# Gate and up of a ConvFFN as seven block products (Strassen) on normalised activations, with u and the residual stored to DRAM before the down product

## The chip, the cores and the metric

The kernel runs on one core of one Trainium2 chip. The metric is device time in microseconds (us) of one execution. The profile of an execution names the engines PE (TensorE matmul), PEld (its weight load), DVE (VectorE), ACT (ScalarE), POOL (GpSimd) and SP (SyncE, which here issues all DMAs, in one order).

## The reference

One decoder layer for 1024 prompt positions and 8 sequences of 8 new positions. Both are carried side by side as N = 1088 columns of a transposed activation: eight tiles of 128 model rows by 1088 columns (D = 1024). All arithmetic is fp32. Cut to what matters here:

```python
x = x + concat([a, o], -1) @ w_out            # a: convolution heads, o: attention heads
h = rms_norm(x, norm_ffn_g)
g_full = concat([ffn_past, h @ w_ffn_gate], 1)
g = depthwise_conv_valid(g_full, ffn_conv_w, ffn_conv_b)      # width 3, causal
x = x + (silu(g) * (h @ w_ffn_up)) @ w_ffn_down               # D_FF = 2816
y = rms_norm(x, norm_final_g)
```

The last two rows of `g_full` of each sequence are an output too (`cf`).

## The kernel before

**Matmuls.** An fp32 product is made of three passes in a rounded fp32 type (`F32R`): each operand is split into hi (a rounded copy, made on ACT) and lo (operand minus hi), and hi·hi, hi·lo and lo·hi are added up in PSUM. `gemm` (L154) does this with a weight tile of 128 output rows: for each of three chunks of columns (`CHUNKS`: 384, 384, 320) and each of the `nk` tiles of 128 input rows there are three matmuls (L167, L168, L169), a triple. After a chunk an eviction is called.

**Weights.** `load_w` (L134) loads a raw weight tile by a DMA from SP (L138; tag WR, two buffers), makes hi on ACT (L141) and lo on POOL (L143). hi and lo come from one set of five buffers (tag W); a buffer is free when the last matmul that reads it is done.

**Output projection.** `out_part` (L764) multiplies `mixed` (attention and convolution outputs, kept in DRAM) by `w_out` in three parts of the input rows (`PARTS`: 3, 3 and 2 tiles). Each part loads its tiles of `mixed` (`load_mixed`, L234), splits them on ACT (L237) and DVE (L238), and adds its product from PSUM to the residual tiles `x2` (L779, DVE). The third part is called at L811.

**Norm.** Behind it `scaled_split` (L223) makes hi (L226, ACT) and lo (L228, DVE) of `x2` times the norm's gain, `h2` (L814), and `sum_squares` and `rstd` (L177) make the norm's column factor `R2` (L815): sums over the partitions on PE (L184), the reciprocal root on DVE and ACT (L188 to L199), transposes back on PE (L206) and a copy on ACT (L208). `R2` is multiplied in when gate and up are evicted from PSUM, so the gate product starts on `h2` before `R2` exists.

**FFN.** `ffn_tile(j)` (L821) does 128 of the 2816 FFN rows: gate weights and up weights by `load_w`, gate product, eviction times `R2` (L833, L835), three taps of the convolution on DVE (L843, L846), silu on ACT (L848), up product, eviction (L855), product (L872, L873), and the split of u (hi on ACT L875, lo on DVE L877). u stays in SBUF as hi and lo. `down` (L880) multiplies a group of up to three such tiles by `w_down` for all eight rows of model tiles and adds it to `x2` (L886). The loop at L910 goes over the groups `QSPLIT` (3, 3, 3, 3, 3, 2, 2, 3) and puts the down product of each group behind the first tile of the next. The last group's product (`last_product`, L924) runs column chunk by column chunk (`TAIL`), with the final norm (`last_norm`, L945) and the stores behind it.

**What sets the order.** The program is written in one sequence. A list scheduler decides from it, with its own model of durations, the order of the instructions of each engine; each engine then runs its list strictly in order. Tags of pools hand out buffers in turn, and an instruction that needs a buffer waits until its last readers are done.

In the branch for the convolution heads earlier in the kernel, the taps (`conv_steps`, L326, L328) run on DVE while POOL splits weights; the prediction takes prices from there.

## Time and profile before

| | us |
|---|---|
| median of 3 runs | 1441.66 |
| lowest, highest | 1438.82, 1442.91 |
| the profiled execution, device time | 1440.49 |
| its span in the profile | 1438.7 |

The mean granted TensorE clock over the profiled execution was 0.987 of full speed. In the page's 40 slices of the span (36 us each) the busy tenths are as follows; the FFN begins in slice 18 of 40.

```profile
PE   7989999999999999999999999999999999999995
DVE  7398695566674666586534534534544544544467
ACT  5312111557564564252111111111111111111134
POOL 3221112010010016132223223223223223232235
PEclk9999999999999999999999999999999999999997
DMA  7237676656698785221112012012011011120203
```

A row of a timeline reads: start in us, duration in us, engine, line, operation, output tile <- input tiles, shape, and in brackets what the engine waited for ahead of it. A row of the costliest groups reads: line, engine, operation, output <- inputs and shapes, count | busy time in all in us, mean ns of one | idle time ahead of them, by what ended it. In a table by stage each pair after the length is busy time and count of PE, PEld, DVE, ACT and POOL; then come the granted clock, the DMA engines' mean busy share, and the GB/s they moved.

### The profile page before, as it was taken

To read this page: it belongs to the slowest core of one execution; us is meant where nothing else is said; L and a number is where in the kernel's file an instruction comes from. 1 tells how busy PE (TensorE), PEld (TensorE's weight loads), DVE (VectorE), ACT (ScalarE), POOL (GpSimd) and SP (SyncE) were. 2 spreads that over 40 slices of the span, in tenths; PEclk is the share of its full clock that TensorE was granted. 3 is DMA by queue.
4 is the path that set the end of the run, shared out by engine and by line. 5 is a ranking of instruction groups with operands and counts; after the bars stand their busy time and mean duration, and the time that the engine had idled before them with its cause. 6 is when DMAs were issued, how large, how long until landed. Compare 5 with 4: busy or idle time off the path is not lost.

```text
span 1438.7 us, 23412 instructions
## 1 busy us (share of the span) xinstructions
PE 1391.2 (97%) x9408; PEld 1327.0 (92%) x9408; DVE 817.3 (57%) x1631; ACT 430.1 (30%) x887; POOL 344.5 (24%) x297
## 2 busy tenths in 40 slices
PE   7989999999999999999999999999999999999995
PEld 7989889999977778999999999999999999999995
DVE  7398695566674666586534534534544544544467
ACT  5312111557564564252111111111111111111134
POOL 3221112010010016132223223223223223232235
PEclk9999999999999999999999999999999999999997
DMA  7237676656698785221112012012011011120203
GB/s 270 61 131 266 223 261 195 189 159 178 174 273 251 214 241 204 82 75 38 31 43 66 25 43 73 18 48 68 18 56 60 18 57 37 41 70 11 70 29 125
DMA packets 75340, 161.64 MB, mean 112 GB/s; under 512 B 12000, under 2 KB 46176, under 8 KB 75232
## 3 DMA queue, kind: packets, MB, share of 16 engines
q1 hardware_dynamic: 75232, 160.15, 36.2%
q8 instruction: 74, 1.21, 0.3%
q14 instruction: 34, 0.28, 0.1%
HBM read 128.32 MB, written 31.81 MB: 111 GB/s over the span
## 4 chain that ended last, share of the span: by engine, by line
PE 84%; DVE 9%; DMA 4%; issue 1%; ACT 1%; SPq 1%; POOL 1%; POOLq 0%; DVEq 0%; ACTq 0%
PE g L167 23%; PE g L169 23%; PE g L168 22%; DVE cacc L326 4%; PE o L659 3%; PE s L574 3%; PE t L642 2%; DVE cacc L328 1%; DMA kk<-dk 1%; PE ss L493 1%; DVE qkv L374 1%; DMA cr<-in_kc 1%; DVE xl L228 1%; PE ss L467 1%; PE g L930 1%
## 5 line engine op out<-in xcount | busy, mean ns | idle before, releaser
L167 PE MATMUL g<-xh,wh 128*128 128x384 f32 x1528 | 502.2, 329 | 1.7 <-DVE x L779 1.7
L168 PE MATMUL g<-xl,wh 128*128 128x384 f32 x1528 | 501.0, 328 | 0.0
L169 PE MATMUL g<-xh,wl 128*128 128x384 f32 x1528 | 498.8, 328 | 0.0
L143 POOL TENSOR_TENSOR wl<-wr,wh 128x1024 fp32r<-128x1024 f32 (+3 forms) x148 | 243.4, 1645 | 880.2 <-PE g L169 742.5
L141 ACT ACTIVATE wh<-wr 128x1024 fp32r<-128x1024 f32 (+3 forms) x150 | 112.8, 752 | 602.1 <-PE g L169 481.1
L167 PEld LDWEIGHTS g<-xh,wh 128*128 128x128 f32 x1528 | 288.0, 189 | 3.4 <-ACT wh L141 1.9
L169 PEld LDWEIGHTS g<-xh,wl 128*128 128x128 f32 x1528 | 287.6, 188 | 2.0 <-issue 1.8
L168 PEld LDWEIGHTS g<-xl,wh 128*128 128x128 f32 x1528 | 288.1, 189 | 1.1 <-issue 1.0
L886 DVE TENSOR_TENSOR x<-g,x 128x384 f32<-128x384 f32 x168 | 89.4, 534 | 117.6 <-PE g L169 115.6
L168 PE MATMUL g<-al,wh 128*128 128x384 f32 (+1 forms) x456 | 149.5, 328 | 0.0
L167 PE MATMUL g<-ah,wh 128*128 128x384 f32 (+1 forms) x456 | 149.5, 328 | 0.0
L169 PE MATMUL g<-ah,wl 128*128 128x384 f32 (+1 forms) x456 | 147.3, 328 | 0.0
L833 DVE TENSOR_TENSOR gb<-g,rb 128x384 f32<-128x384 f32 (+1 forms) x66 | 33.6, 512 | 139.5 <-PE g L169 134.7
L615 ACT ACTIVATE y<-y,m 128x128 f32<-128x128 f32 (+1 forms) x192 | 88.4, 463 | 33.7 <-DVE m L603 33.7
L855 DVE TENSOR_TENSOR u<-g,rb 128x384 f32<-128x384 f32 (+1 forms) x66 | 35.1, 533 | 109.8 <-PE g L169 109.8
L578 DVE CUSTOM_DVE_ANT_0 y<-s,pmk 128x128 f32<-128x128 f32 (+1 forms) x192 | 63.9, 378 | 43.1 <-PE s L574 34.1
L167 PEld LDWEIGHTS g<-ah,wh 128*128 128x128 f32 x456 | 85.8, 188 | 0.0
L168 PEld LDWEIGHTS g<-al,wh 128*128 128x128 f32 x456 | 85.7, 188 | 0.0
L169 PEld LDWEIGHTS g<-ah,wl 128*128 128x128 f32 x456 | 85.5, 188 | 0.0
L326 DVE SCALAR_TENSOR_TENSOR cacc<-gp,prm,cacc 128x1024 f32<-128x1024 f32 x60 | 79.9, 1332 | 0.1
L374 DVE TENSOR_TENSOR qkv<-g,rb 128x384 f32<-128x384 f32 (+1 forms) x53 | 41.1, 775 | 46.1 <-PE g L169 46.0
L167 PE MATMUL g<-mh,wh 128*128 128x384 f32 (+1 forms) x192 | 64.1, 345 | 1.7 <-ACT mh L237 1.7
(197 smaller groups left out, 1925.1 us busy)
## 6 DMA issues: line engine op xcount, KB each, us to landing
cr<-in_kc SPq DMA_DIRECT2D x24, 768.0 KB, 8.7
cr<-in_vc SPq DMA_DIRECT2D x24, 768.0 KB, 7.1
kk<-dk SPq DMA_DIRECT2D x48, 256.0 KB, 7.1
wr<-in_w_in SPq DMA_DIRECT2D x22, 512.0 KB, 5.0
wr<-in_w_gate SPq DMA_DIRECT2D x22, 512.0 KB, 3.5
wr<-in_w_up SPq DMA_DIRECT2D x22, 512.0 KB, 3.5
wr<-in_w_down SPq DMA_DIRECT2D x40, 192.0 KB, 2.3
qs<-dq SPq DMA_DIRECT2D x24, 256.0 KB, 4.1
```

The lines of the kernel that those rows point to most:

```text
L141: nc.scalar.activation(hi, raw, AF.Copy)
L143: lo_eng.tensor_sub(lo, raw, hi.bitcast(F32))
L167: nc.tensor.matmul(ps[c], whi[:, k, :], xh[:, t0:t0 + n], start=(k == 0), stop=False)
L168: nc.tensor.matmul(ps[c], whi[:, k, :], xl[:, t0:t0 + n], start=False, stop=False)
L169: nc.tensor.matmul(ps[c], wlo[:, k, :], xh[:, t0:t0 + n], start=False, stop=(k == nk - 1))
L326: eng.scalar_tensor_tensor(acc[:, :S], gp[:, j:j + S], col(w0 + j), acc[:, :S], op0=ALU.mult, op1=ALU.add)
L374: nc.vector.tensor_mul(by_class(x)[:, t0 // 4:(t0 + m) // 4, :], ps[:, :m].rearrange("p (j c) -> p j c", c=4), R[:, t0:t0 + m].rearrange(" ...
L574: nc.tensor.matmul(ps[:, o:o + n], qq, k[a], start=(a == 0), stop=(a == 1))
L578: nc.vector.tensor_tensor_reduce(out=y[:, o:o + n], in0=ps[:, o:o + n], in1=mask, op0=ALU.add, op1=ALU.min, scale=1.0, scalar=3e38, accum_ ...
L615: nc.scalar.activation(y, y, AF.Exp, bias=m[:, 4 * g + i:4 * g + i + 1], scale=-1.0, accum_out=den[:, g, 2 * hd + u, i:i + 1])
L659: done[x].append(nc.tensor.matmul(dst, v, m, start=not done[x], stop=(left[x] == 0)).ins)
L886: nc.vector.tensor_add(x[:, t0:t0 + n], ps[:, :n], x[:, t0:t0 + n])
```

## The change

Three things change.

**Gate and up by seven products.** Rows and columns are cut in two halves: FFN tile j and tile j + 11 are the two row blocks of the weights A, the first and last four tiles of the model rows their column blocks, and the 1088 columns are two halves of 544 (`HN`). With B the normalised activation, Strassen's method in Winograd's form takes, for a pair of tiles, seven products of blocks in place of eight: b11·a11, t2·s2, b21·a12, t1·s1, t3·s3, b22·s4 and t4·a22, with sums and differences t1 to t4 of the activation's blocks, made once, and s1 to s4 of the weights' blocks, made for each pair (`weight_blocks`: four DVE sums). `block_product` runs one product as 2 chunks of 272 columns x 4 tiles x 3 matmuls into a PSUM pair of two banks (four such pairs). Partial results are added up in PSUM or, with the copies `ta` and `tb`, at eviction on DVE (`put`, `put_u`). The gate's first tap goes from DVE to ACT.

**The norm is multiplied in ahead.** The third part of the output projection runs by column halves (`out_half`: half 0 of all eight tiles, then half 1), with its own weights held whole, and `mixed` loaded in halves. Squares go to ACT, their sums to POOL and DVE. `scale_half` multiplies `x2` by the gain and the norm's factor on DVE. The blocks are split, hi on ACT, lo on POOL (b11, b21, b22, t1, t4) or on DVE (t2, t3).

**u and x2 pass through DRAM.** Each finished `x2` half is stored to DRAM (`x2d`) and each finished tile of u too (`ud`). The down product follows as a phase of its own in four groups of `GROUPS` (6, 6, 6 and 4 tiles of u): `load_act` loads and splits u anew, `reload` brings x2 back, and `load_last` loads the last group's weights. Pools F and D replace pool F, and `rstd`'s column of ones is 128 x 1.

```diff
-QSPLIT = (3, 3, 3, 3, 3, 2, 2, 3)
+GROUPS = ((0, 3), (3, 3), (6, 3), (9, 2))
+HN = N // 2
+HF = NF // 2
+PO = 240
...
-        out_part(*load_part(PARTS[-1], zbig, lambda s: zt("F", "X", 16, s, N, F32R)))
-        h2 = [scaled_split(x2[k], col(C_GFFN + k)) for k in range(KT)]
-        R2 = rstd(sum_squares(x2, nc.vector, zbig), D, zbig)
+        def block_product(o, w, x, start):
+            whi, wlo = w
+            nk = len(x)
+            for c in range(2):
+                n = HN // 2
+                ps = o[:, PO:512] if c == 0 else o[:, 512:PO + HN]
+                for k, (xh, xl) in enumerate(x):
+                    t = slice(c * n, c * n + n)
+                    nc.tensor.matmul(ps, whi[:, k, :], xh[:, t], start=(start and k == 0), stop=False,
+                                     skip_group_check=True)
+                    nc.tensor.matmul(ps, whi[:, k, :], xl[:, t], start=False, stop=False, skip_group_check=True)
+                    nc.tensor.matmul(ps, wlo[:, k, :], xh[:, t], start=False, stop=(k == nk - 1),
+                                     skip_group_check=True)
...
+        def out_half(h):
+            acc = [None, None]
+            c = slice(h * HN, h * HN + HN)
+            for i, m in enumerate(order):
+                ps = pair()
+                block_product(ps, wl[m], part[h], True)
+                x = x2[m][:, c]
+                nc.vector.tensor_add(x, all_of(ps), x)
+                nc.sync.dma_start(x2d[m][:, c], x)
+                s = slot("t1", "sq", F32)
+                nc.scalar.activation(s, x, AF.Square)
...
+        def scale_half(h, sq):
+            r = rstd(sq, D, lambda s: slot("b22", s, F32), HN)
+            for k in order:
+                x = x2[k][:, h * HN:h * HN + HN]
+                nc.vector.scalar_tensor_tensor(x, x, col(C_GFFN + k), r, op0=ALU.mult, op1=ALU.mult)
+                if h == 0:
+                    tag = "b11" if k < 4 else "b21"
+                    blocks[tag].append(split(x, tag, nc.gpsimd))
+        sq0 = out_half(0)
+        scale_half(0, sq0)
+        scale_half(1, out_half(1))
+        for k in range(4):
+            (x11, x12), (x21, x22) = halves(x2[k]), halves(x2[k + 4])
+            nc.vector.tensor_sub(x11, x12, x11)
+            blocks["b22"].append(split(x22, "b22", nc.gpsimd))
+            nc.vector.tensor_sub(x12, x22, x12)
+            nc.vector.tensor_sub(x22, x22, x11)
+            nc.vector.tensor_sub(x21, x21, x22)
+            blocks["t2"].append(split(x22, "t2", nc.vector))
+            blocks["t1"].append(split(x11, "t1", nc.gpsimd))
+        for k in range(4):
+            blocks["t3"].append(split(halves(x2[k])[1], "t3", nc.vector))
+            blocks["t4"].append(split(halves(x2[k + 4])[0], "t4", nc.gpsimd))
...
+        def weight_blocks(w, j):
...
+            g, u = raw(j), raw(j + HF)
+            a11, a12 = parts(g, [zt("F", "WA", 2, "wa", D, F32R) for _ in range(2)])
+            t = wide("w22")
+            a22, = parts(u[:, half:], (t[:, :half], t[:, half:]))
+            g1, g2, u1, u2 = g[:, :half], g[:, half:], u[:, :half], u[:, half:]
+            nc.vector.tensor_add(u2, u1, u2)
+            nc.vector.tensor_sub(u1, g1, u1)
+            nc.vector.tensor_sub(g1, u2, g1)
+            nc.vector.tensor_sub(g2, g2, g1)
+            s2, s4 = parts(g, [wide("s24") for _ in range(2)])
+            s3, s1 = parts(u, [wide("s31") for _ in range(2)])
+        def products(w, j, c11, put):
+            a11, a12, a22, s1, s2, s3, s4 = weight_blocks(w, j)
+            x, y = pair("px"), pair("py")
+            block_product(x, a11, blocks["b11"], True)
+            ta = zt("F", "tmp", 4, "ta", HN)
+            nc.scalar.activation(ta, all_of(x), AF.Copy)
+            block_product(y, s2, blocks["t2"], True)
+            put(1, 0, y, ta)
+            block_product(x, a12, blocks["b21"], False)
+            c11(x)
+            block_product(y, s1, blocks["t1"], False)
+            tb = zt("F", "tmp", 4, "tb", HN)
+            nc.vector.tensor_add(tb, all_of(y), ta)
+            z = pair("pz")
+            block_product(z, s3, blocks["t3"], True)
+            put(1, 1, z, tb)
+            block_product(y, s4, blocks["b22"], False)
+            put(0, 1, y, ta)
+            block_product(z, a22, blocks["t4"], False)
+            put(1, 0, z, None)
...
-            nc.vector.tensor_scalar(cvt[:, :W], gb[:, 0:W], col(C_FW + 3 * j), col(C_FB + j),
-                                    op0=ALU.mult, op1=ALU.add)
+                nc.scalar.activation(c[:, :W], gb[i][:, 0:W], AF.Identity, bias=col(C_FB + f), scale=col(C_FW + 3 * f))
...
+                    nc.sync.dma_start(ud[j], u[0])
...
+        def load_act(j0, n):
+            act = []
+            for i in range(2):
+                for j in range(j0 + i * HF, j0 + i * HF + n):
+                    raw = zt("D", "XR", XF, "ur")
+                    nc.sync.dma_start(raw, ud[j])
+                    hi, lo = wide("ah", F32R), wide("al", F32R)
+                    nc.scalar.activation(hi, raw, AF.Copy)
+                    nc.vector.tensor_sub(lo, raw, hi.bitcast(F32))
+                    act.append((hi, lo))
+            return act
```

Where the instructions stand now, at the places that the prediction speaks of. A row is line, operation, output <- inputs, shape; numbers behind a name tell tiles apart.

PE at the FFN's norm, before: `g` is a gate or up product in PSUM, `r` the norm's sums.

```order
L169 MATMUL g_7063<-xh_6878,wl_6971 128x384
L184 MATMUL r_6921<-ones,sqa_6898 128x1 x8
L184 MATMUL r_6921<-ones,sqa_6898 64x1
L167 MATMUL g_7063<-xh_6882,wh_6969 128x384
L168 MATMUL g_7063<-xl_6884,wh_6969 128x384
```

PE there in the change: `g_6789` is the last row block of half 0 of the output projection, `g_6875` the first of half 1.

```order
L841 MATMUL g_6789<-mh_6641,wl_6631 128x272
L189 MATMUL g_1258_6808<-ones,sq_6680 128x1 x4
L189 MATMUL g_1258_6808<-ones,sq_6680 32x1
L211 MATMUL g_1263_6826<-ident,rr_6818 128x128 x4
L211 MATMUL g_1264_6832<-ident,rr_6818 128x32
L838 MATMUL g_6875<-mh_6647,wh_6623 128x272
```

The norm's passes stood between gate matmuls; now half 0's stand, in one piece, ahead of half 1's first matmul.

DVE at the same place in the change: `rb_6825` is half 0's norm factor, the L902 rows are its multiplications into `x2`, the L887 rows the evictions of half 1.

```order
L204 SCALAR_TENSOR_TENSOR rr_6818<-rt_6821,rr_6818 128x5
L191 MEMSET rv_14012 128x2
L902 SCALAR_TENSOR_TENSOR x_1099_5934<-x_1099_5934,prm,rb_6825 128x544
L902 SCALAR_TENSOR_TENSOR x_1127_6094<-x_1127_6094,prm,rb_6825 128x544
L902 SCALAR_TENSOR_TENSOR x_1106_5974<-x_1106_5974,prm,rb_6825 128x544
L902 SCALAR_TENSOR_TENSOR x_1134_6134<-x_1134_6134,prm,rb_6825 128x544
L902 SCALAR_TENSOR_TENSOR x_1113_6014<-x_1113_6014,prm,rb_6825 128x544
L902 SCALAR_TENSOR_TENSOR x_1141_6174<-x_1141_6174,prm,rb_6825 128x544
L902 SCALAR_TENSOR_TENSOR x_1120_6054<-x_1120_6054,prm,rb_6825 128x544
L902 SCALAR_TENSOR_TENSOR x_1148_6214<-x_1148_6214,prm,rb_6825 128x544
L887 TENSOR_TENSOR x_1099_5934<-g_6875,x_1099_5934 128x544
L887 TENSOR_TENSOR x_1127_6094<-g_6892,x_1127_6094 128x544
```

Before, no multiplication stood there; evictions (L779) alternated with the lo splits (L228).

DVE between the gate and the up half of a pair, in the change: `gb` is the gate's result, `fc` the convolution's, `py` and `pz` PSUM pairs of the gate (9384, 9487) and of up (9604, 9605).

```order
L1010 TENSOR_TENSOR gb_9354<-py_9384,ta_9409 128x480
L1011 TENSOR_TENSOR gb_9354<-py_9384,ta_9409 128x8x8
L1008 TENSOR_TENSOR gb_9355<-pz_9487,gb_9355 128x544
L1022 SCALAR_TENSOR_TENSOR fc_9567<-gb_9354,prm,fc_9567 128x1104 x2
L1022 SCALAR_TENSOR_TENSOR fc_9574<-gb_9355,prm,fc_9574 128x1104 x2
L1038 TENSOR_TENSOR u_9580<-py_9605,ta_9630 128x544
L1034 TENSOR_TENSOR u_9579<-px_9604,fc_9567 128x544
L976 TENSOR_TENSOR tb_9706<-py_9605,ta_9630 128x544
```

Before, two taps of one tile (L846) stood between a gate's evictions and up's; now four stand there.

SP at the end of gate and up, in the change: `u_7152` to `u_7173` and `x2d` are tiles in DRAM, `ur` the raw tiles of u that are loaded again.

```order
L1041 DMA u_7162<-u_11759 128x1088
L1075 DMA x_1801_12465<-x2d_6663 128x1088
L143 DMA wr_12255<-in_w_down 128x2x384
L1066 DMA ur_11979<-u_7152 128x1088
L1066 DMA ur_11985<-u_7153 128x1088
L1066 DMA ur_11991<-u_7154 128x1088
L1075 DMA x_1748_12089<-x2d_6658 128x1088
L1044 DMA u_7173<-u_11760 128x1088
L1075 DMA x_1808_12533<-x2d_6664 128x1088
L1066 DMA ur_11997<-u_7163 128x1088
```

Before, SP had only weight loads there; stores and loads of u and x2 now stand between them.

247 lines of the change are left out of this document (159 added, 88 removed).

## The prediction

> **What bounds the kernel now.** I read the page's busy shares and its chain of waits first, then a table by stage, then the timeline around the stage that changes.
>
> ```profile
> span 1438.7 us, 23412 instructions
> PE 1391.2 (97%) x9408; PEld 1327.0 (92%) x9408; DVE 817.3 (57%) x1631; ACT 430.1 (30%) x887; POOL 344.5 (24%) x297
> PE 84%; DVE 9%; DMA 4%; issue 1%; ACT 1%; SPq 1%; POOL 1%; POOLq 0%; DVEq 0%; ACTq 0%
> ```
> ```profile
> 599.30:627.60 28.30, 25.96 (x145) 25.33 (x144) 23.50 (x30) 16.57 (x20) 9.69 (x8) 0.94 0.26 86
> 627.60:1360.00 732.40, 731.18 (x4436) 730.83 (x4437) 344.57 (x461) 130.30 (x153) 190.47 (x185) 1.00 0.15 45
> ```
>
> The second fence has one row a stage: length, busy time of PE, PEld, DVE, ACT and POOL, granted clock, DMA. From 628 us on PE never rests and DVE is busy 47%, POOL 26%: time there is the number of matmuls times their pitch. The timeline gives the pitch by the start of every third matmul, all of one line:
>
> ```profile
> 646.00 0.33 PE L167 MATMUL g<-xh,wh 128*128 128x384 f32 x1
> ...
> 649.12 0.33 PE L167 MATMUL g<-xh,wh 128*128 128x384 f32 x1
> 652.91 0.31 PE L167 MATMUL g<-xh,wh 128*128 128x320 f32 x1
> ...
> 655.55 0.31 PE L167 MATMUL g<-xh,wh 128*128 128x320 f32 x1
> 1388.75 0.28 PE L930 MATMUL g<-ah,wh 128*128 128x256 f32 x1
> ...
> 1397.69 0.28 PE L930 MATMUL g<-ah,wh 128*128 128x256 f32 x1
> 1418.44 0.28 PE L932 MATMUL g<-ah,wl 128*128 128x256 f32 x1
> ```
>
> 18 matmuls of 384 columns in 3.12 us are 0.1733 us each, 18 of 320 in 2.64 are 0.1467, 75 of 256 in 8.94 are 0.1192: a straight line, on which 272 columns cost 0.126. The last row is the last matmul of the last product, near 1418.5; the tail behind it, 20.2 us, does not change.
>
> **What is removed.** Gate and up were 22 x 2 x 8 x 3 triples (three chunks, three products of hi and lo): 2112 matmuls of 384 (366.0) and 1056 of 320 (154.9), 520.9 us. Now 22 sets (11 pairs, gate and up) have 7 x 4 x 3 x 2 = 168 matmuls of 272: 3696 x 0.126 = 465.7. So 55.2 us go, less than the eighth that the method saves in columns, since each matmul's fixed part is paid oftener. Down: 18 x 8 x 3 triples of chunk matmuls now (213.1) and a last product over 4 tiles (48.4), 261.5, against 19 x 8 x 3 (224.9) and 36.3, 261.2: +0.3. The first norm's sums and transposes between gate matmuls took some 3.6 us of PE; they move ahead of the products.
>
> **What the change puts in their place: the opening.** Before, gate starts on unnormalised x2, R2 being multiplied in at eviction. Now the products need normalised, combined and split blocks. Prices:
>
> ```profile
> 88.61 1.26 DVE L326 SCALAR_TENSOR_TENSOR cacc<-gp,prm,cacc 128x1024 f32<-128x1024 f32 x1
> 89.79 2.44 DVE L328 SCALAR_TENSOR_TENSOR cacc<-se,prm,cacc 128x64 f32<-128x64 f32 x1
> 93.35 0.28 DVE L328 SCALAR_TENSOR_TENSOR cacc<-se,prm,cacc 128x64 f32<-128x64 f32 x1
> 89.31 2.83 POOL L143 TENSOR_TENSOR wl<-wr,wh 128x1024 fp32r<-128x1024 f32 x1 [9.35 <-PE g L169]
> 619.15 1.87 DVE L779 TENSOR_TENSOR x<-g,x 128x384 f32<-128x384 f32 x4
> 618.28 1.55 POOL L143 TENSOR_TENSOR wl<-wr,wh 128x256 fp32r<-128x256 f32 x1 [1.81 <-PE g L169]
> 638.10 1.34 DVE L228 SCALAR_TENSOR_TENSOR xl<-x,prm,xh 128x1088 fp32r<-128x1088 f32 x1
> 639.36 1.28 DVE L220 TENSOR_TENSOR sqa<-sq,sqa 128x1088 f32<-128x1088 f32 x1
> ```
> ```profile
> L143 POOL TENSOR_TENSOR wl<-wr,wh 128x1024 fp32r<-128x1024 f32 x44 | 105.5, 2397 | 279.9 <-PE g L169 275.9 <-ACT wh L141 4.0
> L143 POOL TENSOR_TENSOR wl<-wr,wh 128x384 fp32r<-128x384 f32 x46 | 48.0, 1044 | 208.0 <-PE g L169 166.5 <-issue 41.4
> L846 DVE SCALAR_TENSOR_TENSOR fc<-gb,prm,fc 128x1104 f32<-128x1104 f32 x44 | 62.0, 1410 | 1.5
> L141 ACT ACTIVATE wh<-wr 128x1024 fp32r<-128x1024 f32 x43 | 45.6, 1061 | 220.2 <-PE g L169 151.8 <-DMA wr<-in_w_gate 48.5 <-DMA wr<-in_w_up 13.7
> ```
>
> The first four rows carry the forecast. POOL's split asks at 89.31, waits for the running DVE operation, then holds a DVE operation of 0.28 us for 2.44: its own 2.4. A POOL operation and a DVE operation with two SBUF inputs do not run together; each waits for the other's end, in turn, though DVE had the next one queued. DVE adds that read PSUM (619.15) run beside POOL. Lengths for 544 columns, on lines through these rows: POOL 1.38, DVE 0.64 start to start for a sum or difference, 0.70 with a scalar (starts lie 0.08 closer than durations).
>
> By the order shown with the change, PE holds half 0's sums and transposes ahead of half 1's first matmul (before, gate matmuls stood around them), and DVE holds all eight normalisations of half 0 (L902) ahead of half 1's evictions (L887), while POOL's eight splits of b11 and b21 alternate with them; with four PSUM pairs PE must stop at the fifth row block. The timeline at the same place before:
>
> ```profile
> 599.04 0.31 PE L169 MATMUL g<-mh,wl 128*128 128x320 f32 x1
> 601.01 1.11 PE L167 MATMUL g<-mh,wh 128*128 128x384 f32 x5 [1.66 <-ACT mh L237]
> 602.34 0.52 PE L168 MATMUL g<-ml,wh 128*128 128x384 f32 x1 [0.22 <-DVE ml L238]
> 602.66 0.52 PE L169 MATMUL g<-mh,wl 128*128 128x384 f32 x1
> 606.52 0.34 PE L168 MATMUL g<-ml,wh 128*128 128x384 f32 x1
> 628.82 0.41 PE L167 MATMUL g<-xh,wh 128*128 128x384 f32 x1 [1.68 <-DVE x L779]
> 642.87 2.05 PE L184 MATMUL r<-ones,sqa 128*128 128x1 f32 x18
> 646.11 0.17 DVE L199 SCALAR_TENSOR_TENSOR rr<-rt,rr 128x9 f32<-128x9 f32 x1
> 650.45 1.09 ACT L208 ACTIVATE rb<-r 128x512 f32<-128x512 f32 x2 [4.78 <-PE r L206]
> ```
>
> The walk, on the old clock. The last third of the output projection starts at 601; after that 1.7 us rest PE runs at half rate (0.32 between 602.34 and 602.66) until 606.5, a loss of some 2.5. Now its loads of mixed stand in SP's queue behind a gate weight that waits for POOL, and the lo parts of mixed wait for a POOL split: 605.1 for the first full triple. 24 matmuls at half rate (5.5) and 68 at 0.126 (8.6): half 0 ends at 619.2. Last eviction, square and two sums (2.7), ten short PE passes (1.2), reciprocal root (1.35, as 644.9 to 646.3), transposes and copy (1.5): DVE normalises from 626.1.
>
> From there to the last t2 split DVE and POOL take turns. DVE: 16 normalisations (11.2) and 28 sums, differences and splits (17.9). POOL: 22 of 544 columns (30.4: b11 and b21, squares, b22, t1, three of t4) and three weight splits (7.2). Together 66.7, plus 7.3 in which both wait for the second norm: 74, to 700. In it PE does half 1 and 106 product matmuls (b11, b21, most of t3, b11 of up). Behind it 3590 matmuls are left: 452.3, with 2.5 for the half-rate restart and 2 for two evictions (into t1, b22) that nothing covers now.
>
> Bounds: if POOL and DVE ran side by side the 74 shrink by 28 (the first rival); if turns go worse, one more POOL operation behind each of the second eight normalisations (the first eight are already paired), 11 more. I take 74, since the rows at 89 us show it operation by operation.
>
> [...]
>
> **The steady sets.** 21.2 us of PE a set. W's five buffers hold one set, so the next set's splits wait for products of this one: w22 for t1 (ACT 0.6, POOL 1.3), then four DVE sums (2.6), s2's hi (1.1), and its lo once b22 is done (2.4): ready some 8.6 us after t1 ends, due 11.5 after it (three further products and most of b21). That cover holds. The tightest place is DVE between the two halves of a pair. By the order shown, the gate's four taps (L1022) stand ahead of up's first eviction (L1038), which must have read py before t1 adds to it. From the end of the gate's last product to t1's turn PE has 9.2 us of other products (b21, t2, t3); DVE needs the gate's last eviction 0.65, then the rest of POOL's split of s3 and s1 (1.8, the taps read SBUF twice), four taps (4 x 1.33 by the L846 row), three small POOL copies in turn (0.6) and up's eviction 0.65: 9.0. Nothing is left for a late hand-over. I take 0.3 a pair, 3; bounds 0 and 22 (2 a pair: a whole weight split between the taps, less what slack there is).
>
> **The way through DRAM.** At the end of gate and up, by SP's order shown, a w_down load (wr_12255) that waits for a raw buffer stands ahead of the first reload of u (ur_11979), and the last store of u (u_7173) ahead of the fourth. POOL frees that buffer with m = 1's split, about when the last product ends. The nearest rows for a load of 544 KB:
>
> ```profile
> mx<-mixed SPq DMA_DIRECT2D x8, 544.0 KB, 5.4
> xr<-in_xT SPq DMA_DIRECT2D x8, 544.0 KB, 3.9
> ```
>
> Before, u never left SBUF. Now the first tile lands 3.9 to 5.4 after the last product, and is split in 1.1 on ACT and 1.3 on DVE: PE rests some 6.5, and about 1 more for later tiles, of which each feeds 15 matmuls (2.5 us); with 2.5 for the restart at half rate I take 10. Bounds 4 (the loads start a product earlier) and 18 (the nine transfers of 544 KB around it one after the other, half a load each). The u stores and the x2 store and reload otherwise lie beside products: DMA was busy 15% of this stage, and 22 stores and 22 loads of 544 KB at 3.9 are spread over 460 us. If that cover failed, it would show as the same wait at each group.
>
> [...]
>
> **Sum.** 700 + 2.5 + 2 + 452.3 + 3 = 1159.8; +10; +261.5, and 4.0 for the tail norms (what 628.8 to 1418.5 holds beyond 520.9, 261.2 and 3.6) = 1435.3; +20.2 = 1455.5 of span, against 1438.7. The profiled execution took 1440.49, 1.8 over its span, and the median lies 1.2 higher: **1459**, 1.2% slower. The 55 us come back in the opening and at the DRAM crossing.
>
> **Rivals.**
> 1. Faster (0.14): in the opening POOL and DVE run side by side. Then normalisation ends by 632, PE doesn't stop in half 1, and the last split comes near 672: 28 earlier, **1431**. For it: DVE's adds from PSUM do run beside POOL. Against: rows 89.79 and 93.35. It decides once 22 of the 74 us vanish. [...]
> 2. Much slower (0.18): a weight split of 2.4 falls between the four taps in every pair; t1 waits some 2 us in 11 pairs, **1478 to 1481**. For it: no slack there; against: that split is due only after b21 of up.
> 3. Matmuls don't get cheaper below 320 columns (0.03): 3696 at 0.147 are 543 us, **1536**. Against: 0.1192 at 256.
>
> **Chances and range.** The forecast has 0.65 and by itself covers 1445 to 1474 (opening 66 to 85, crossing 4 to 18). A measurement here can't tell changes under 0.3% (4.3 us). Faster takes rival 1, 0.14; the forecast's lower edge gives 0.06 to "same"; the rest, 0.80, is slower. The range that leaves out two in ten: 1436 to 1484.
>
> **What would show it.** Right: PE idle in several pieces between about 620 and 700, DVE normalisations of 2 us beside POOL splits, a second pitch of 0.126 from 700 to 1160 with PE nearly full, and one gap of 6 to 8 us before the down product with ur loads at its end. Wrong: products in full stride before 680, py evictions late in every pair, or no gap at the crossing.

## The result, and the profile after

| | before | changed |
|---|---|---|
| median, us | 1440.02 (12 runs) | 1449.28 (12 runs) |
| lowest to highest | 1435.45 to 1447.19 | 1443.70 to 1456.03 |
| the profiled execution, its span | 1440.49, 1438.7 | 1453.19, 1451.3 |

The ratio is 1.0063, 95% interval 1.0043 to 1.0083: slower, by 9.3 us where 17.3 were forecast (1459 against the 1441.66 of the three runs known then). The page's head and the shares of the chain of waits of the changed kernel:

```profile
span 1451.3 us, 24741 instructions
PE 1355.6 (93%) x10011; PEld 1286.5 (89%) x10011; DVE 860.0 (59%) x1619; ACT 515.3 (36%) x978; POOL 473.1 (33%) x330
PE 74%; DVE 13%; DMA 6%; issue 2%; ACT 2%; POOL 2%; SPq 1%; POOLq 0%; ACTq 0%; DVEq 0%
```

PE has 35.6 us less to do than before (1391.2), but holds 74% of the chain, not 84%; of these ten points DVE took four (9% to 13%) and DMA two. The profiled execution lies 3.9 above its median. Its third part begins late for a reason that is not the change's: the last matmul of the second part starts at 602.53, against 599.04 before, after the same PE program, and nearly all of the difference is there by 589 us. In the profiles of the experiments below, which change nothing ahead of it either, it starts between 596.8 and 608.3. So all times below are counted from that matmul, in each kernel's own trace. From there to the end of the span it is 839.7 us before and 848.8 now: +9.1, as the medians say.

The table by stage of the changed kernel, cut at the end of half 0's matmuls, the start and end of the first eight multiplications, the start of the second eight, the last t2 split, and the last gate and up matmul (columns as before):

```profile
622.53:630.01 7.48, 3.01 (x17) 2.58 (x18) 2.94 (x10) 2.83 (x5) 1.23 (x1) 0.77 0.20 74
630.01:641.16 11.15, 7.47 (x48) 7.26 (x46) 11.15 (x9) 4.61 (x7) 9.59 (x6) 0.81 0.01 1
641.16:664.18 23.02, 12.50 (x65) 11.85 (x66) 10.03 (x20) 8.42 (x14) 13.05 (x8) 0.65 0.40 143
664.18:696.31 32.13, 19.08 (x102) 18.28 (x101) 32.12 (x32) 12.94 (x20) 22.10 (x10) 0.68 0.00 1
696.31:722.53 26.22, 23.85 (x184) 22.98 (x183) 16.57 (x17) 11.98 (x13) 19.33 (x20) 1.00 0.13 42
722.53:1102.53 380.00, 380.00 (x3039) 380.00 (x3038) 233.85 (x262) 126.17 (x136) 187.65 (x144) 1.00 0.23 77
1102.53:1150.65 48.12, 47.30 (x377) 47.02 (x376) 30.74 (x35) 14.05 (x15) 19.54 (x13) 1.00 0.37 121
1150.65:1160.19 9.54, 0.15 (x3) 0.01 (x1) 2.27 (x4) 1.95 (x2) 0.30 (x1) 0.76 0.88 308
1160.19:1432.23 272.04, 269.71 (x1693) 268.53 (x1694) 98.72 (x157) 62.38 (x89) 67.83 (x45) 0.99 0.29 92
```

The opening is rows 2 to 4: PE is busy for 39 of 66 us, at 0.65 to 0.81 of its clock, and of 3696 gate and up matmuls 102 are done. Then PE rests hardly at all for 454 us; 3039 matmuls in 380 us are a pitch of 0.1250 at 272 columns. Row 8 is the crossing. The waits of PE from 690 us on (total, how often, the longest):

```profile
PE g L172 <- ACT ah L1068: 9.7, 2, 9.4
PE py L838 <- DVE tb L976: 1.6, 2, 0.8
```

After the 9.4 us of the crossing nothing stands there that recurs in each pair.

| us, from the second part's last matmul | predicted | measured |
|---|---|---|
| until the first multiplication | 27.1 | 27.5 |
| from there to the last t2 split | 73.9 | 66.3 |
| matmuls left x pitch (3590 x 0.126; 3594 x 0.1250) | 452.3 | 449.4 |
| lost beside them | 7.5 | 4.8 |
| from gate and up's last matmul to the last product's | 275.5 | 281.6 |
| tail | 20.2 | 19.2 |
| sum | 856.5 | 848.8 |

The timeline of DVE and POOL in the opening shows the turns, and where they stop:

```profile
630.01 11.15 DVE L902 SCALAR_TENSOR_TENSOR x<-x,prm,rb 128x544 f32<-128x544 f32 x8 [1.98 <-ACT rb L213]
664.18 7.83 DVE L902 SCALAR_TENSOR_TENSOR x<-x,prm,rb 128x544 f32<-128x544 f32 x8 [1.98 <-ACT rb L213]
671.94 7.24 DVE L912 TENSOR_TENSOR x<-x 128x544 f32<-128x544 f32 x4
694.96 1.35 DVE L872 TENSOR_TENSOR t2l<-x,t2h 128x544 fp32r<-128x544 f32 x2
631.57 1.83 POOL L872 TENSOR_TENSOR b11l<-x,b11h 128x544 fp32r<-128x544 f32 x1 [7.80 <-ACT b11h L871]
650.04 2.55 POOL L942 TENSOR_TENSOR s<-wr,s 128x1024 fp32r<-128x1024 f32 x1 [3.73 <-ACT s L941]
652.55 1.81 POOL L894 TENSOR_TENSOR sq<-sq,sq 128x544 f32<-128x544 f32 x1
656.62 1.32 POOL L894 TENSOR_TENSOR sq<-sq,sq 128x544 f32<-128x544 f32 x1
691.36 7.50 POOL L872 TENSOR_TENSOR t4l<-x,t4h 128x544 fp32r<-128x544 f32 x2 [6.43 <-ACT t4h L871]
```

While POOL splits b11 and b21 (1.8 us each; 1.36 for the split at 643.64, where DVE rests), eight multiplications take 11.15 us, and beside the splits of b22 and t1 the four L912 differences take 1.8 each. At 691.36 it is otherwise: POOL's split of t4 comes while DVE is in a row of sums and splits of 0.635 us, and gets no turn before DVE's row ends at 696.3; two splits take 7.50.

### The profile page after: what moved, and what is told of

The parts are those of the page before. It is cut to its first block, busy times and chain, and to the rows that moved or that the text cites. A ratio compares the mean times of both kernels' runs of the same rounds, so it can differ in the third digit from the quotient of the medians.

```text
span 1451.3 us, 24741 instructions
## 1 busy us (share of the span) xinstructions
PE 1355.6 (93%) x10011; PEld 1286.5 (89%) x10011; DVE 860.0 (59%) x1619; ACT 515.3 (36%) x978; POOL 473.1 (33%) x330
## 4 chain that ended last, share of the span: by engine, by line
PE 74%; DVE 13%; DMA 6%; issue 2%; ACT 2%; POOL 2%; SPq 1%; POOLq 0%; ACTq 0%; DVEq 0%
PE g L174 9%; PE g L172 9%; PE g L173 9%; PE py L838 4%; PE py L840 4%; PE py L841 4%; DVE cacc L331 4%; PE o L664 3%; PE s L579 3%; PE pz L841 3%; PE pz L838 3%; PE pz L840 3%; PE px L838 3%; PE px L840 3%; PE px L841 3%
## 5 line engine op out<-in xcount | busy, mean ns | idle before, releaser
L148 POOL TENSOR_TENSOR wl<-wr,wh 128x768 fp32r<-128x768 f32 (+2 forms) x63 | 121.7, 1933 | 472.7 <-PE g L174 357.8
L172 PE MATMUL g<-xh,wh 128*128 128x384 f32 (+1 forms) x472 | 158.5, 336 | 0.0
L173 PE MATMUL g<-xl,wh 128*128 128x384 f32 (+1 forms) x472 | 157.0, 333 | 0.0
L174 PE MATMUL g<-xh,wl 128*128 128x384 f32 (+1 forms) x472 | 156.8, 333 | 0.0
L942 POOL TENSOR_TENSOR s<-wr,s 128x1024 fp32r<-128x1024 f32 x44 | 107.6, 2446 | 88.1 <-ACT s L941 45.4
L172 PEld LDWEIGHTS g<-ah,wh 128*128 128x128 f32 x432 | 81.7, 191 | 11.6 <-ACT ah L1068 10.2
L174 PEld LDWEIGHTS g<-xh,wl 128*128 128x128 f32 x472 | 89.6, 190 | 2.0 <-issue 1.8
L172 PEld LDWEIGHTS g<-xh,wh 128*128 128x128 f32 x472 | 89.8, 190 | 1.4 <-issue 1.2
L173 PEld LDWEIGHTS g<-xl,wh 128*128 128x128 f32 x472 | 90.0, 191 | 1.1 <-issue 1.0
L1022 DVE SCALAR_TENSOR_TENSOR fc<-gb,prm,fc 128x1104 f32<-128x1104 f32 x44 | 79.7, 1831 | 1.6 <-ACT fc L1020 0.9
L942 POOL TENSOR_TENSOR wa<-wr,wa 128x1024 fp32r<-128x1024 f32 x22 | 57.3, 2603 | 53.9 <-ACT wa L941 53.8
```

Of the source, the lines that this page charges most:

```text
L148: lo_eng.tensor_sub(lo, raw, hi.bitcast(F32))
L172: nc.tensor.matmul(ps[c], whi[:, k, :], xh[:, t0:t0 + n], start=(k == 0), stop=False)
L173: nc.tensor.matmul(ps[c], whi[:, k, :], xl[:, t0:t0 + n], start=False, stop=False)
L174: nc.tensor.matmul(ps[c], wlo[:, k, :], xh[:, t0:t0 + n], start=False, stop=(k == nk - 1))
L942: nc.gpsimd.tensor_sub(lo, x, hi.bitcast(F32))
L1022: nc.vector.scalar_tensor_tensor(c[:, :W], gb[i][:, t:t + W], col(C_FW + 3 * f + t), c[:, :W], op0=ALU.mult, op1=ALU.add)
```

## The experiments

Fifteen kernels, each against the changed kernel (1449.28) unless it is said otherwise. "Gate/up end" is the start of the last gate and up matmul, "last" that of the down product's last one, both counted as above. By the intervals shown, two rows of 12 runs are told apart when their ratios differ by some 0.003, which is 4 us.

| | median (runs) | ratio to before, 95% | last t2 split | gate/up end | last |
|---|---|---|---|---|---|
| the changed kernel | 1449.28 (12) | 1.0063, 1.0043 to 1.0083 | 93.8 | 548.0 | 829.6 |
| e1 all splits on DVE | 1454.21 (6) | 1.0091, 1.0064 to 1.0118 | 83.1 | 549.8 | 830.0 |
| e2 factor from PSUM | 1445.65 (12) | 1.0033, 1.0013 to 1.0053 | 88.5 | 541.8 | 824.7 |
| e3 sums on DVE | 1449.40 (8) | 1.0062, 1.0035 to 1.0089 | 91.9 | 546.0 | 827.8 |
| e4 early reload of u | 1449.73 (6) | 1.0068, 1.0042 to 1.0095 | 94.4 | 548.8 | 830.3 |
| e5 halves first | 1448.13 (12) | 1.0046, 1.0027 to 1.0064 | 89.7 | 544.5 | 826.4 |
| e6 e4, x2 behind u | 1441.23 (12) | 1.0011, 0.9990 to 1.0031 | 93.8 | 547.9 | 822.2 |
| e7 opening hollow | 1410.09 (4) | 0.9789, 0.9770 to 0.9808 | | 511.4 | 791.0 |
| e8 no first reload | 1440.00 (10) | 0.9992, 0.9972 to 1.0011 | 93.7 | 547.9 | 821.0 |
| e9 e1 in another form | 1451.72 (8) | 1.0064, 1.0043 to 1.0086 | 82.8 | 548.5 | 828.6 |
| e10 e2 and e6 | 1439.70 (12) | 0.9981, 0.9959 to 1.0002 | 88.6 | 541.9 | 816.4 |
| e11 e10, POOL relieved | 1441.42 (12) | 1.0005, 0.9983 to 1.0028 | 80.2 | 546.9 | 822.4 |
| e12 e11, halves first | 1440.53 (12) | 0.9991, 0.9971 to 1.0011 | 76.1 | 542.4 | 817.8 |
| e13 e9 with a column | 1455.60 (6) | 1.0103, 1.0078 to 1.0127 | 85.4 | 551.3 | 832.2 |
| e14 e12 with a column | 1440.17 (12) | 0.9995, 0.9972 to 1.0018 | 79.0 | 546.8 | 822.8 |
| e15 e12, plain form, one split moved | 1428.86 (6) | 0.9912, 0.9885 to 0.9939 | 78.1 | 532.1 | 805.9 |

**What the two places cost in all: e7 and e8.**

```diff
-            r = rstd(sq, D, lambda s: slot("b22", s, F32), HN)
-                nc.vector.scalar_tensor_tensor(x, x, col(C_GFFN + k), r, op0=ALU.mult, op1=ALU.mult)
...
+        for tag in ("t2", "t1", "t3", "b22", "t4"):
+            blocks[tag] = blocks["b11"]
```

> Left out: both norm factors, all sixteen multiplications, all sums and differences of the activation's blocks and the splits of t2, t1, t3, b22 and t4; the seven products all read the split, unnormalised blocks of half 0. PE's matmuls, the weights' sums and splits, the evictions and both passes through DRAM stay. Theory A (the steady sets run at their matmuls' pace, 465.7 us, and all else that gate and up lost lies in the opening): gate and up end 44 to 49 us earlier, counted from the second part's last matmul, and so does the time. Rival B (weight blocks, taps or evictions hold the sets up too): 35 us or less.

```diff
+            if j0 == 0:
+                hi, lo = wide("ah", F32R), wide("al", F32R)
+                nc.vector.memset(hi.bitcast(F32), 0.0)
+                nc.vector.memset(lo.bitcast(F32), 0.0)
+                return [(hi, lo)] * (2 * n)
```

> Left out: the first group's six reloads of u and their twelve splits; the first group of the down product reads two zeroed tiles instead. The stores of u, the reloads of x2 and the other groups stay. Theory A (the crossing costs its gap of 9.7, the half rate behind it, 2.9, and waits of 2 at the next tiles): the time falls by 11 to 15 us against the changed kernel. Rival B (what is won is lost again a few us on, to the weights or the second group's reloads, as in e4): 5 us or less.

e7: 39.2 us faster, gate and up end 36.6 earlier: between the two theories. The table by stage of e7 from its first to its last gate and up matmul, and its waits:

```profile
629.30:1109.00 479.70, 469.84 (x3697) 464.31 (x3696) 289.22 (x320) 154.36 (x170) 246.29 (x177) 1.00 0.24 80
```
```profile
PE py L841 <- POOL s L930: 5.8, 12, 0.7
PE py L838 <- DVE u L1026: 2.8, 11, 0.3
```

Without the opening the sets took 479.7 us, 17.7 more than 3696 x 0.1250 = 462.0; PE now waits a little for weight blocks in 12 of the 22 sets (0.5 us each), which the changed kernel does not. So e7 gives the opening's price from below: 37 to 39 us, and what its hidden second limit swallows. e8: 9.3 us faster, short of the 11 to 15 expected, and nearer to A than to B. From gate/up end to last it takes 273.1 us, 8.5 less; 265.5 were forecast for that stretch without a crossing, so 7.6 remain that are not the reloads'. The waits of PE in e8 name 4.7 of these: 2.2 for the zeroed tiles, which e8 itself put there, and 1.8 and 0.7 for hi and lo of the weights at the start of the last product. Without e8's own 2.2 us the gain would be some 11.5 us, an estimate from this wait, and within A.

**Who sets the opening: e1, e2, e3, e5.**

```diff
-                    blocks[tag].append(split(x, tag, nc.gpsimd))
+                    blocks[tag].append(split(x, tag, nc.vector))
...
-            blocks["b22"].append(split(x22, "b22", nc.gpsimd))
+            blocks["b22"].append(split(x22, "b22", nc.vector))
```

> All twenty lo parts of the opening (b11, b21, b22, t1, t4) move from POOL to DVE; nothing else changes. Theory A (POOL and DVE take turns, a pair of operations costs 1.8 us, two DVE operations 1.3): the eight multiplications of half 0 take 5.5 us, not 11.2, PE's stop of 4.4 us in half 1 goes, the second norm comes some 8 us earlier, the last t2 split comes 8 to 14 us earlier (counted from the third part's first matmul), and the time falls by 8 to 14 us against the changed kernel. Rival B (the two run beside each other, DVE's own list is the bound): DVE's list grows by 20 x 0.64 = 12.8 us and the time rises by 8 to 13 us. Rival C (PE's own work and the norm's chain set the opening): within 3 us.

```diff
-            r = rstd(sq, D, lambda s: slot("b22", s, F32), HN)
+            r = rstd(sq, D, None, HN)
...
+            if new is None:
+                pb = zone["Fps"].tile([P, 1024], F32, tag="g2", name=nm("pr"), bufs=4)
+                for i, n in enumerate(size):
+                    nc.tensor.transpose(pb[:, i * P:i * P + n], r[:n, i:i + 1].to_broadcast([n, P]), ident[:n, :n])
+                return pb[:, :width]
```

> The norm's factor stays in PSUM, so that the sixteen multiplications (x times gain times factor) read one operand from SBUF and one from PSUM; ACT's copy to SBUF goes. Theory A (it is the second SBUF operand that makes DVE and POOL wait for each other): eight multiplications take 5.8 us, not 11.2 and 7.8, POOL's splits beside them 1.36 each, not 1.8; PE's stop of 4.4 us in half 1 goes; time falls by 4 to 8 us against the changed kernel. Rival B (POOL slows DVE whatever DVE reads, or a PSUM operand is slower here): multiplications stay at 1.4 us each, and time stays within 2 us.

```diff
-                    (nc.vector if i % 2 else nc.gpsimd).tensor_add(acc[i % 2], s, acc[i % 2])
+                    nc.vector.tensor_add(acc[i % 2], s, acc[i % 2])
```

> POOL's six sums of squares in the opening move to DVE; nothing else changes. Theory A (the second norm waits for a sum that stands on POOL behind two weight splits): the second norm's sums come 4 to 6 us earlier and the time falls by 3 to 6 us against the changed kernel. Rival B (what follows is set by POOL's later splits, so an earlier norm buys nothing): within 2 us.

```diff
-        sq0 = out_half(0)
-        scale_half(0, sq0)
-        scale_half(1, out_half(1))
+        sq0, sq1 = out_half(0), out_half(1)
+        scale_half(0, sq0)
+        scale_half(1, sq1)
```

> Both column halves of the output projection's third part are written ahead of both normalisations, so that PE does half 1 right behind half 0 and DVE evicts half 1 ahead of the first multiplication. Theory A (what is dear in the opening is that the norm of half 0 and eight multiplications stand between the halves): the last matmul of the third part comes at about 33 us after the second part's last one, not 47.7, the second multiplications some 15 us earlier; DVE's 44 operations and the POOL turns among them stay, so the last t2 split comes at 82 to 87 us, not 93.8, and the time falls by 6 to 12 us against the changed kernel. Rival B (the volume of DVE and POOL work sets the end of the opening, the order only moves the waits): within 3 us.

The timeline of POOL and DVE in e2, with the factor read from PSUM:

```profile
629.09 1.35 POOL L877 TENSOR_TENSOR b11l<-x,b11h 128x544 fp32r<-128x544 f32 x1 [7.50 <-ACT b11h L876]
627.54 5.62 DVE L907 SCALAR_TENSOR_TENSOR x<-x,prm,pr 128x544 f32<-128x544 f32 x8 [1.50 <-PE pr L208]
655.44 5.62 DVE L907 SCALAR_TENSOR_TENSOR x<-x,prm,pr 128x544 f32<-128x544 f32 x8 [1.51 <-PE pr L208]
```

The same eight multiplications take 5.62 us, not 11.15 and 7.83, beside POOL splits of 1.35 to 1.39: theory A of e2. Gate and up end 6.2 earlier and the time falls by 3.6, just short of the 4 to 8 expected and at the edge of what the intervals tell apart. e1 also freed the multiplications (5.66), and the last t2 split came 10.7 us earlier, inside theory A; but the time did not fall as A had it: the median is 4.9 higher, which the intervals do not tell from no change, and gate and up end 1.8 later. The timeline of e1 shows why: POOL has one weight split left there, for up's first set.

```profile
669.16 21.71 POOL L942 TENSOR_TENSOR wa<-wr,wa 128x1024 fp32r<-128x1024 f32 x1 [15.26 <-ACT wa L941]
668.27 0.71 DVE L872 TENSOR_TENSOR b22l<-x,b22h 128x544 fp32r<-128x544 f32 x1
686.04 2.63 DVE L872 TENSOR_TENSOR t4l<-x,t4h 128x544 fp32r<-128x544 f32 x4
```
```profile
PE px L841 <- POOL gb L998: 11.6, 1, 11.6
```

2.4 us of work take 21.7: POOL waits while DVE works through 31 operations without a pause, up to 688.7, and PE then rests 11.6 us for it. The waits name the next POOL operation (gb), which waits behind the split. e3 brought the last t2 split 1.9 us forward and no time that can be told (its rival B). e5 brought half 1's last matmul from 47.7 to 32.1, but the eight multiplications of half 0, still 11.07 us beside POOL, then stand in DVE's order ahead of the second norm's small operations, and PE waits 13.5 us for these. The median is 1.2 us lower, which is no change that can be told and lies within the rival's bound. The timeline of DVE and the wait of PE in e5:

```profile
649.10 11.07 DVE L902 SCALAR_TENSOR_TENSOR x<-x,prm,rb 128x544 f32<-128x544 f32 x8 [1.35 <-ACT rb L213]
660.10 0.15 DVE L193 TENSOR_SCALAR rv<-g 128x4 f32<-128x4 f32 x1
```
```profile
PE g L211 <- DVE rv L191: 19.1, 2, 13.5
```

**The crossing: e4, e6.**

```diff
+        zt("D", "XR", XF, "layout")
         acts = [load_act(*GROUPS[0])]
...
-                    nc.sync.dma_start(raw, ud[j])
+                    (nc.scalar if j < XF else nc.sync).dma_start(raw, ud[j])
```

> At the crossing: the raw buffers for the reloaded u lie over b11, which is read last 15 us before gate and up end, not over b22 and t4, and the first three reloads are issued from ACT's queue, not from SP's behind a store of u that waits for DVE and a weight load that waits for POOL. Theory A (the queue sets the gap): the first reload is issued some 4 us earlier (by the end of the weight splits on ACT), PE's gap of 9.7 us falls to 5 to 6, and the time falls by 3 to 5 us against the changed kernel. Rival B (the nine transfers of 544 KB around it share the DMA engines, and the time from issue to landing grows by what is won): the gap stays over 8 us and the time within 2 us.

```diff
-                    nc.sync.dma_start(raw, ud[j])
+                    d = (nc.scalar if j < XF else nc.sync).dma_start(raw, ud[j])
+                    if j0 == 0:
+                        behind[:] = [d.ins]
...
-            nc.sync.dma_start(x2[m], x2d[m])
+            with tc.issue_after(behind[0]):
+                nc.sync.dma_start(x2[m], x2d[m])
```

> As e4 (early raw buffers, first three reloads of u from ACT's queue), and the eight reloads of x2 are issued only behind the six reloads of u. Theory A (at the crossing PE waits for the sixth tile of u, and the 4.4 MB of x2 that share the DMA engines with it are what holds it up): PE's first gap is 4 us as in e4, the second stop of some 6 us that e4 showed shrinks to 2 or less, and the time falls by 5 to 8 us against the changed kernel. Rival B (the three raw buffers, each of which waits for DVE's split, hold the later tiles up): the second stop stays and the time is within 2 us.

The timeline of PE in e4 behind the last gate and up matmul, and the wait of PE in e6:

```profile
1157.42 1.11 PE L172 MATMUL g<-ah,wh 128*128 128x384 f32 x5 [3.46 <-ACT ah L1068]
1173.15 1.92 PE L172 MATMUL g<-ah,wh 128*128 128x384 f32 x5 [5.77 <-ACT ah L1068]
```
```profile
PE g L172 <- ACT ah L1072: 3.6, 1, 3.6
```

In e4 the gap falls from 9.4 to 3.5 us, and 10 us after its end PE stops for 5.8: the first three tiles came early, the next three did not, and no time was won, as rival B had it, though its gap of over 8 us is not there. In e6 the second stop is gone, the time falls by 8.1, and gate/up end to last by 7.2: theory A at its upper edge. The rows of the fourth tile of u, first its issue and then its hi split, in e4 and in e6, and the wait of SP in e4:

```profile
1162.95 3.01 SPq L1066 DMA_DIRECT2D ur<-u  x3
1171.98 1.11 ACT L1068 ACTIVATE ah<-ur 128x1088 fp32r<-128x1088 f32 x1 [10.18 <-DMA ur<-u]
1149.84 4.70 SPq L1068 DMA_DIRECT2D ur<-u  x3
1155.98 1.11 ACT L1072 ACTIVATE ah<-ur 128x1088 fp32r<-128x1088 f32 x1 [3.17 <-DMA ur<-u]
```
```profile
SPq L1075 <- DMA u<-u: 8.5, 2, 5.2
```

e4's second stop ends with the split of the fourth tile (1171.98 + 1.11, PE at 1173.15), not of the sixth that the expectation named. Counted from gate/up end (1153.68 in e4, 1144.63 in e6), that tile's reload is issued at 9.3 and 5.2 us and has landed at 18.3 and 11.3. So of the 7.0 us won 4.1 are the order of SP's queue, where a reload of x2 that waits 5.2 us for a store of u stands ahead of it, and 2.9 are a shorter time from issue to landing. The theory had only the second of these, and all 4.4 MB of x2; by SP's timeline four of the eight reloads of x2 were issued 11 to 18 us ahead of gate/up end, in the changed kernel and in e4, and in e4 the DMA engines were idle again from 1146 to 1151. The gap that is seen first is not the price.

**Why a shorter opening did not move the end: e9 to e15.** e10 puts e2 and e6 together; e11 also moves the sums of squares and the splits of b22, t1 and t4 to DVE and writes DVE's sums and splits in e9's form; e12 adds e5's order; e15 is e12 with plain sums and splits, as in e1, and one weight split moved.

```diff
+        def minus(o, a, b):
+            nc.vector.scalar_tensor_tensor(o, a, 1.0, b, op0=ALU.mult, op1=ALU.subtract)
...
-            nc.vector.tensor_sub(x11, x12, x11)
+            minus(x11, x12, x11)
```

> As e1 (all opening splits on DVE), but DVE's sums, differences and splits of the opening are written as SCALAR_TENSOR_TENSOR (operand times 1.0 minus operand) in place of TENSOR_TENSOR. In e1 POOL's weight split that came to DVE's stream at 669 us waited for the end of the whole stream, 19.5 us, and PE for it, 11.6 us. Theory A (a POOL operation that arrives anew gets its turn behind the running operation in a stream of SCALAR_TENSOR_TENSOR, and none in a stream of TENSOR_TENSOR): the weight split takes under 5 us, PE's wait of 11.6 goes, gate and up end 6 to 11 us earlier than in e1, and the time is 5 to 10 us below e1's 1454.2. Rival B (POOL waits for a gap in DVE's stream, whatever its operations): the split takes over 15 us again and the time is within 3 us of e1's.

> e2 and e6 together: the norm's factor read from PSUM; reloads of u early and from ACT's queue, those of x2 behind them. If opening and crossing are two separate prices, the gains add: 3.6 + 8.1 = 11.7 us below the changed kernel's 1449.3, about 1437 to 1439. If a gain in the opening is eaten behind it (the rival), it stays at e6's 1441.

> e10, and in the opening the squares' sums and the splits of b22, t1 and t4 go from POOL to DVE, with DVE's sums and splits as SCALAR_TENSOR_TENSOR. Theory (POOL is the engine that e2's chain of waits names behind the second norm, and DVE has room there): the last t2 split by 82 us after the second part's last matmul, gate and up end by 536, and the time falls to 1428 to 1433. Rival (DVE's own list is then the bound, or the order moves a stop from one half to the other, as in e5): 1436 to 1440.

> e11, with both halves of the third part ahead of both normalisations as in e5. Theory (in e5 the second norm stood behind eight multiplications of 11.1 us, which now take 5.8): the second norm is ready some 12 us earlier than in e11, the last t2 split by 72 us, and the time falls a further 4 to 8 us, to 1422 to 1428. Rival (as in e5, the order only moves the stops): within 2 us of e11.

e9: the split took 21.2 us again, so the type of operation does not decide who gets a turn:

```profile
664.03 21.23 POOL L948 TENSOR_TENSOR wa<-wr,wa 128x1024 fp32r<-128x1024 f32 x1 [15.74 <-ACT wa L947]
```

e10: 9.6 of the 11.7 us; the two prices add within the intervals. e11 brought the last t2 split to 80.2, within the 82 expected, and e12 to 76.1, short of the 72 expected; but gate/up end came no earlier than e10's 541.9, and the times are those of the rivals or above. The waits of PE in e12:

```profile
PE pr L208 <- DVE rv L191: 13.3, 2, 7.6
PE px L846 <- POOL gb L1009: 11.6, 1, 11.6
PE py L843 <- ACT t2h L876: 8.4, 1, 8.4
```

The second row is e1's stop once more. Three runs were made for what was then open: what lets POOL in, and whether the one shut-out split is all that holds the end. The first cut below is against e9, the second against the changed kernel.

```diff
-            nc.vector.scalar_tensor_tensor(o, a, 1.0, b, op0=ALU.mult, op1=ALU.subtract)
+            nc.vector.scalar_tensor_tensor(o, a, ones, b, op0=ALU.mult, op1=ALU.subtract)
```

> As e9, with the 1.0 of DVE's sums and splits read from a column in SBUF (128 x 1), as the multiplications and the taps read theirs. In all traces so far a POOL operation that came to a stream of operations with such a column (start to start 0.70 us) got its turn at once, and one that came to a stream without it (0.635) waited to the end. Theory A (the column leaves the gap that lets POOL in): starts 0.70 apart, the weight split takes under 5 us, PE's wait of 11.6 goes, time 1443 to 1447. Rival B (something else lets POOL in, such as what the operation before it waited for): the split takes over 15 us again, time 1449 to 1454.

> e12 with the column of e13. Theory A: the weight split of up's first set gets in, PE's wait of 11.6 us there goes, gate and up end by 535 us after the second part's last matmul, time 1430 to 1435. Rival B (as in e13, no turn): as e12, 1438 to 1443.

```diff
+            def parts(x, new, eng=nc.gpsimd):
...
-                nc.gpsimd.tensor_sub(lo, x, hi.bitcast(F32))
+                eng.tensor_sub(lo, x, hi.bitcast(F32))
...
+            a11, a12 = parts(g, [zt("F", "WA", 2, "wa", D, F32R) for _ in range(2)],
+                             nc.vector if w is w_up and j == 0 else nc.gpsimd)
```

> e12 with plain sums and splits, and the one weight split that starved (the lo part for up's first set) moved into DVE's list. Theory A (that split, shut out by DVE's stream, is what PE waits for): the wait of 11.6 us goes, gate and up end by 535 us, time 1430 to 1435, whatever e13 shows. Rival B (that wait only covers another one, for t2 or the gate's own weights): within 3 us of e12's 1440.5.

The timeline of POOL and DVE in e13:

```profile
671.81 23.98 POOL L948 TENSOR_TENSOR wa<-wr,wa 128x1024 fp32r<-128x1024 f32 x1 [15.17 <-ACT wa L947]
671.94 0.78 DVE L879 SCALAR_TENSOR_TENSOR x<-x,ones 128x544 f32<-128x544 f32 x1
672.64 0.78 DVE L879 SCALAR_TENSOR_TENSOR b22l<-x,ones,b22h 128x544 fp32r<-128x544 f32 x1
```

Starts lie 0.70 us apart, as with the multiplications, and POOL is shut out for longer still; the column only made DVE slower (starts 0.635 apart in e9). Theory A of e13 and e14 falls (e14: 1440.17, as e12), and what lets POOL in beside the multiplications of the norm, and not beside these sums and splits, stays open. What it does to the time is settled by e15. With that one split in DVE's own list PE's wait of 11.6 us is gone; the longest waits that are left are these:

```profile
PE pr L208 <- DVE rv L191: 13.3, 2, 7.6
PE py L843 <- ACT t2h L876: 9.0, 1, 9.0
```

Gate and up end at 532.1, 10.3 before e12, and the time is 1428.86: 11.7 below e12, and below both kernels, at 0.9912 (0.9885 to 0.9939) of the time before. e15 also goes back to the plain form of the sums and splits; by e1 and e9, which differ in that form alone (1454.21 and 1451.72, not told apart), the form is not what won it.

## Why the prediction was right in direction and wrong in size

- **Removed.** Right. The pitch at 272 columns is 0.1250, not 0.126; gate and up's matmuls take 462.0 us (3696 x 0.1250) where 465.7 were forecast, 58.9 less than before.
- **The opening: the step that failed.** The prediction put it so: "From there to the last t2 split DVE and POOL take turns", 66.7 us "plus 7.3 in which both wait for the second norm: 74". It measured 66.3, and the sum came that near by luck, since two errors offset each other: 20.8 us too much for turns, 15.7 too little for the wait. Of DVE's 44 operations 40 stand in two streams and take 26.5 us by themselves: 5.66 for the first eight, as in e1, and 20.84 for the rest (8 x 0.70 + 24 x 0.635); the other four, sums of squares, fall into the wait. Turns were priced at 37.6 (25 POOL operations); DVE lost 16.8 to them, 11.15 less 5.66 in the first stream and 32.13 less 20.84 in the second. The wait for the second norm was priced at 7.3 and is 23.0, row 3 of the table by stage. 26.5 + 16.8 + 23.0 = 66.3. In these 23 us PE finishes half 1 (its last matmul starts at 650.19, after a stop of 4.4 us and a restart at half rate, 0.226 a matmul until 647.0), the last sum of squares on POOL stands behind two weight splits and ends at 657.9, and the small steps of the norm follow. The prediction had put half 1 beside the turns. Eight of POOL's operations (squares, weight splits, the last splits of b11 and b21) fall into this wait, in which DVE mostly waits or reads PSUM, and the three of t4 that were counted found no turn before DVE's stream ended. So 14 turns were left of 25, and each cost DVE 1.1 to 1.2 us, not 1.38 (a weight split 2.1, not 2.4). That turns exist, and that the second SBUF operand makes them, e2 shows: 5.62 us against 11.15 for the same work.
- **In turn, operation by operation.** Right from 631 to 641 and from 666 to 685, also for splits that came anew while the multiplications ran (631.57, 666.43). Wrong at 691, and in e1, e9 and e13, where DVE goes on and POOL is shut out. In the changed kernel that favoured the end of the opening (t2 is on DVE) and cost little, since t4 is used last; in e1 it cost 11.6 us of PE.
- **Behind the opening.** 3594 matmuls were left, 3590 forecast. 4.8 us were lost beside them, not 7.5: 380 us in the middle of the sets show no idle time at all, so the stall between the taps, which had 0.3 us a pair, does not show there.
- **The crossing.** Under-sized: 275.5 forecast from the last gate and up matmul to the last matmul, 281.6 measured. PE rests 9.4 us where 6.5 were forecast, and runs at half rate up to 1166.1 (0.32 us a matmul of 384 columns, 0.175 behind that). Waits of 1.8 us for weights at the start of the last product (1.1 for ACT's hi, 0.7 for POOL's lo) were not in the forecast. The step named the queue; e4 and e6 show that its order and the transfers around the fourth tile set the price, not its first load. In the changed kernel the stores of u and x2 cost nothing that shows, as forecast.
- **The rivals.** Rival 1, POOL and DVE side by side, is refuted by the 11.15 us and by e2. Rival 2 by the idle-free sets. Rival 3 by the pitch.
- **Sums that do not come out.** The steps ahead of the first multiplication add up to 625.95, not 626.1; the five terms of the next set's splits to 8.0, not 8.6; and with POOL and DVE side by side the 74 would lose DVE's 29.1, not 28. None of them moves the forecast by more than 0.2 us.
- **Net.** -7.6 in the opening, -2.9 by the pitch, -2.7 behind it, +6.1 at the crossing and after, -1.0 in the tail, +0.4 ahead of the opening: 7.7 less than forecast.

## What to carry to other kernels

A method that saves matmuls pays for its operands in the stage ahead of them: here 59 us of PE were saved and some 68 lost, most of it in two places where PE had been busy (39.2 went with the opening in e7, 9.3 with the reloads in e8). Count such an opening from the engine that waits, stretch by stretch, and not as a sum of two engines' work: of the 25 POOL operations counted as turns, only the 14 that fell into DVE's two streams cost one. A single POOL operation of 2.4 us that DVE's stream shut out held PE for 11.6 us (e1, e12); moving it into DVE's list removed that stop (e15), and reading one operand from PSUM removed the turns of the multiplications (e2, 5.62 us for 11.15). A stop that is first in the trace (the gap of e4) is worth only what the next stop leaves.

## What the runs showed that was not expected

A POOL operation with SBUF operands waited for a whole stream of DVE operations: 19.5 us for 2.4 of work in e1, 24.0 in all in e13. In e2 a split of b22 that came at 661.19 to DVE's differences found no turn until DVE itself paused at 668. All this stands against turns of 1.8 us a pair elsewhere in the same kernel. Neither the type of DVE's operations (e9, 21.2 us) nor a scalar column in SBUF (e13) decides it. Behind rests of 3.2 to 9.8 us PE ran at half rate. In the changed kernel's opening this happened five times (from 629.43, 641.85, 663.60, 671.88 and 687.52): 0.226 us a matmul of 272 columns, not 0.125, the last time for 3.9 us, at a granted clock of 0.50; over the whole rows 2 to 4 of the table by stage the clock is 0.65 to 0.81. At the crossing it lasted 5.9 us (from 1160.19, clock 0.51).
